# Hybrid decoder block on one core: the down projection's operand sums move into the FFN loop, and the second norm's gain moves to the weights

## The chip, the cores and the metric

The kernel runs on one core of a Trainium2 chip. The time is device microseconds per execution, median of three runs. PE is the matrix engine (TensorE), PEld its weight loads, DVE VectorE, ACT ScalarE, POOL GpSimd, SP the engine whose queue issues most DMAs.

## The reference

One decoder layer in float32 on x of 1024 tokens x 1024: norm, one input projection, retention heads and differential attention side by side, an output projection, then the FFN that this case is about:

```python
x = x + jnp.einsum('bse,ed->bsd', mix, w_out[l])
h2 = rms_norm(x, norm2_g[l])               # norm2_g: one gain for each of the 1024 columns
ff = jax.nn.silu(h2 @ w_gate[l]) * (h2 @ w_up[l])   # 1024 x 2816 each
x = x + ff @ w_down[l]                     # 2816 x 1024
```

## The kernel before

Every large product is made of three matmuls (`mm3`): a float32 operand is cut into `hi`, a cast by ACT to the matrix engine's rounded float32, and `lo`, the rest, subtracted by DVE; hi x hi, hi x lo and lo x hi are summed in PSUM. `wp` holds the moving operands: 8 buffers each of `whi` and `wlo`, and `NRAW` = 2 of the tag `raw` for sums.

The stages on the time axis: projections, attention and retention to about 480 us; the output projection's first column half; then the *middle stage*, about 500 to 617 us: second half of the output projection, token tile by token tile in the order 0, 4, 1, 5, 2, 6, 3, 7, with norm2 and the first gate product between. Its order is written out by hand: `MID_PLAN` gives for a step of the loop over PE's work the functions that are called there (`n_square`: squares on ACT, their sum on POOL; `n_scale`: x2 times 1/norm times `gtile`, on DVE; `n_turn`: transposes on PE; `n_split`: hi and lo of the turned tile; `f_sum`, `f_split`: the sums of quarter blocks that Strassen needs; `g_weights`, `g_add`: the first gate's), and engines keep the program's order there. Elsewhere the scheduler sets the order.

`blk` 0 to 6 hold the seven left operands of the Strassen scheme, turned (0 to 2 in the pool `act2`, 3 to 6 in `act`). In the FFN, 617 to 1024 us, a `Strassen` takes two 128-column tiles of w_gate or w_up: two 512 KB loads (`rawp`, 3 buffers), seven products of 12 matmuls (four k steps by three), five of them with a sum of weights on POOL. Gate and up alternate, 22 in all; silu on ACT, their product on DVE, and the four 128x512 results of a pair go to DRAM (`ffd`).

Down, 1024.5 to 1256.5 us, is Strassen too: `DOWN` lists seven products (n), each 11 steps (c) of 4 token tiles x 3 matmuls, 132. Its a operand comes from `ffd`, its b operand from w_down; `operand` forms the sum of two blocks on POOL if there is one, then hi on ACT and lo on DVE. Five products have an a-sum and five a b-sum, three of them (n = 2, 3, 6) both. w_down's tiles of two of its four quarters are kept (`kept`, 14 slots), the others loaded for each use (`raw`, 5 buffers of the pool `bp`). After each product DVE adds or subtracts the four PSUM banks to one or two of the accumulators `acc`, which start as x2 read back from `x2d`; finished ones go out.

The line number in most rows of the profile is that of the helper which records operations, so groups go by tile names.

Of the kernel before, what the change touches and what calls it, by code (L numbers as in the profile page):

```python
# [25 lines left out]
NF = DFF // P  # L26
# [25 lines left out]
def constants():  # L52
# [148 lines left out]
    (55, "o_load", 3, 1),  # L201
    (55, "o_add", 3, 1),
    (56, "f_split", 3, 2),
    (57, "g_weights", 1),
    (58, "f_sum", 4, 2, "G"),
    (58, "n_square", 3, 1),
# [53 lines left out]
def block_kernel(ctx: ExitStack, tc: tile.TileContext, x, norm1_g, w_in, ret_norm_g, dq_g, dk_g,  # L260
# [4 lines left out]
    class Pinned:  # L265


        def __init__(self, engine):
            self.engine = engine
# [8 lines left out]
    V, A, G, T = Pinned(nc.vector), Pinned(nc.scalar), Pinned(nc.gpsimd), Pinned(nc.tensor)  # L278

    const = ctx.enter_context(tc.tile_pool(name="const", bufs=1))  # L280
    act = ctx.enter_context(tc.tile_pool(name="act", bufs=4))
    wp = ctx.enter_context(tc.tile_pool(name="wp", bufs=KC))
    st = ctx.enter_context(tc.tile_pool(name="st", bufs=6))
# [5 lines left out]
    ident = cs[:, C_ID:C_ID + P]  # L289
    nhalf = cs[:, C_NHALF:C_NHALF + 8]  # L290
    g1col = const.tile([P, KC], F32, name="g1col")
    ms = const.tile([P, NT], F32, name="ms")
    rs = const.tile([P, NT], F32, name="rs")
    eps1 = const.tile([P, NT], F32, name="eps1")
# [49 lines left out]
    def whole(parts):  # L344
        w = next(parts)
        for _ in parts:
            pass
        return w
# [137 lines left out]
    def small_loads():  # L486
        for g_sb, g_dr in ((gq, dq_g), (gk, dk_g)):
            for m in range(2):
                nc.sync.dma_start(g_sb[m * HD:(m + 1) * HD, :], g_dr[0].rearrange("(d o) -> d o", o=1))
        for i, l_dr in enumerate((lq1, lq2, lk1, lk2)):  # L490
            nc.sync.dma_start(lam4[:, i, :], l_dr[0].partition_broadcast(P))
        nc.sync.dma_start(gout[:, 0:4], ret_norm_g[0].rearrange("h d -> (h d)").rearrange("(k p) -> p k", p=P))
        nc.sync.dma_start(gout[:, 4:5], subln_g[0].rearrange("(d o) -> d o", o=1))

    lsum = const.tile([P, 2], F32, name="lsum")
    lexp = const.tile([P, 2], F32, name="lexp")
# [387 lines left out]
    hps = ctx.enter_context(tc.tile_pool(name="hps", bufs=4, space=bass.MemoryType.PSUM))  # L884
    dram = ctx.enter_context(tc.tile_pool(name="dram", bufs=1, space=bass.MemoryType.DRAM))
    x2d = dram.tile([S, D], F32, name="x2d")
    ffd = dram.tile([NF, P, S], F32, name="ffd")
    apx = ExitStack()
    ap = apx.enter_context(tc.tile_pool(name="ap", bufs=2))
    gtile = ap.tile([P, D], F32, tag="rawp", name="gtile", bufs=3)  # L890
    nc.scalar.dma_start(gtile, norm2_g[0].partition_broadcast(P))

    def bankh():
        return hps.tile([P, 512], F32, tag="h", name="h")
# [31 lines left out]

    def n_scale(t, q):
        h2[t] = x2[t]
        V.scalar_tensor_tensor(out=h2[t][q], in0=x2[t][q], scalar=sums[t][:, 0:1],
                               in1=gtile[:, q * 512:(q + 1) * 512], op0=ALU.mult, op1=ALU.mult)  # L930

    def n_turn(t, q):
        turned[t, q] = turn(h2[t][q])
# [39 lines left out]
    class Strassen:  # L973


        def __init__(self, w, f0, pool, tag):
            self.raw, self.w, self.m, self.out, self.pool, self.tag = [], {}, {}, {}, pool, tag
            for j in range(2):
                r = ap.tile([P, 4, 2, P], F32, tag="rawp", name="rawp", bufs=3)
                nc.sync.dma_start(r.rearrange("p k i e -> p k (i e)"),  # L980
                                  w[0, j * 512:(j + 1) * 512, f0 * P:(f0 + 2) * P].rearrange("(k p) e -> p k e", p=P))
                self.raw.append(r)

        def weights(self, n):
            (i, j), other, op, *_ = PRODUCTS[n]
# [53 lines left out]
    def g_load():  # L1039
        gate.append(Strassen(w_gate, 0, rowb, "rowb"))  # L1040

    def g_weights(n):
        gate[0].weights(n)

# [11 lines left out]
    o_load(0, 1)  # L1056
    order["pinned"] = True
    for step, _ in enumerate(mid()):
        if step == 8 * 6:
            g_load()  # L1060
        for at, f, *args in MID_PLAN:
            if at == step:
                names[f](*args)
# [2 lines left out]
            names[f](*args)  # L1066
    order["pinned"] = False

    for f0 in range(0, NF, 2):
# [11 lines left out]
    bp = ctx.enter_context(tc.tile_pool(name="bp", bufs=1))  # L1081
    NH = NF // 2
    keep = act2.tile([P, 8, 512], F32, tag="act2", name="keep")
    more = act2.tile([P, 8, 512], F32, tag="act2", name="more")
    kept = [keep[:, i, :] for i in range(8)] + [more[:, i, :] for i in range(4)]
    kept += [bp.tile([P, 512], F32, name=f"kept{i}") for i in range(2)]
    ff = [more[:, 4:6, :], more[:, 6:8, :]]
    for f in range(2, NF, 4):
        ft = (act2 if f == 2 else act).tile([P, 4, 2, 512], F32, tag="act2" if f == 2 else "act", name="ff")
        ff += [ft[:, i] for i in range(4)]  # L1090
    acc = [[None, None] for _ in range(NT)]

    def w_get(to, c, j, dh):
        f = 2 * c + j
        nc.sync.dma_start(to, w_down[0, f * P:(f + 1) * P, dh * 512:(dh + 1) * 512])
        return to

    def a_get(c, sh, j):
        f = 2 * c + j
        nc.sync.dma_start(ff[f][:, sh, :], ffd[f, :, sh * 512:(sh + 1) * 512])  # L1100

    def operand(both, x_, y_=None, op=None):
        hi, lo = (wp.tile([P, 512], F32R, tag=tag_, name=tag_) for tag_ in ("whi", "wlo"))
        if y_ is not None:
            G.tensor_tensor(out=both, in0=x_, in1=y_, op=op)
# [6 lines left out]
    DOWN = [(((1, 1), None, None), (1, 1), ((1, 0), (0, 0), ALU.subtract), {(0, 0): 1, (1, 0): 1}, ()),  # L1112
            (((1, 0), (1, 1), ALU.add), (1, 0), ((0, 0), None, None), {(1, 0): 1, (1, 1): -1}, ((1, 0),)),
            (((1, 0), (0, 0), ALU.subtract), (0, 0), ((0, 1), (0, 0), ALU.add), {(1, 1): 1}, ()),
            (((0, 0), (1, 1), ALU.add), None, ((1, 1), (0, 0), ALU.add), {(0, 0): 1, (1, 1): 1}, ()),
            (((0, 0), (0, 1), ALU.add), (0, 1), ((1, 1), None, None), {(0, 0): -1, (0, 1): 1}, ()),
            (((0, 0), None, None), None, ((0, 1), (1, 1), ALU.subtract), {(0, 1): 1, (1, 1): 1}, ((0, 1), (1, 1))),
            (((0, 1), (1, 1), ALU.subtract), None, ((1, 0), (1, 1), ALU.add), {(0, 0): 1}, ((0, 0),))]
    at = {}
    for n, ((a0, a1, aop), new, (b0, b1, bop), outs, done) in enumerate(DOWN):  # L1120
        m = [bankh() for _ in range(4)] if n % 2 == 0 else [bankp(), bankp(), bankm([P, 512]), bankm([P, 512])]
        for c in range(NH):

            b = {}
            for name in (b0, b1):
                if name in ((0, 0), (1, 1)):
                    if (name, c) not in at:
                        at[name, c] = w_get(kept[(c if name == (0, 0) else NH + c) % len(kept)], c, *name)
                    b[name] = at[name, c]
                elif name is not None:  # L1130
                    b[name] = w_get(bp.tile([P, 512], F32, tag="raw", name="raw", bufs=5), c, *name)
            if new is not None:
                a_get(c, *new)
            a = {i: ff[2 * c + i[1]][:, i[0], :] for i in (a0, a1) if i is not None}
            both = aop and bp.tile([P, 512], F32, tag="sum", name="sum", bufs=2)
            ah, al = operand(both, a[a0], a.get(a1), aop)
            both = bop and wp.tile([P, 512], F32, tag="raw", name="sum", bufs=NRAW)
            bh, bl = operand(both, b[b0], b.get(b1), bop)
            for t in range(4):
                mm3(m[t], ah[:, t * P:(t + 1) * P], al[:, t * P:(t + 1) * P], bh, bl, c == 0, c == NH - 1)  # L1140
        if n == 0:
            for sh, dh in ((0, 0), (1, 0), (1, 1), (0, 1)):
                for t in range(4 * sh, 4 * sh + 4):
                    acc[t][dh] = (rowb if dh else rowa).tile([P, 512], F32, tag="rowb" if dh else "rowa", name="acc")
                    nc.sync.dma_start(acc[t][dh], x2d[t * P:(t + 1) * P, dh * 512:(dh + 1) * 512])
        for t in range(4):
            for (sh, dh), sign in outs.items():
                o = acc[4 * sh + t][dh]
# [29 lines left out]
```

## Time and profile before

| | |
|---|---|
| median of 3 runs | 1263.63 us (1262.44 to 1264.25) |
| profiled execution, its own time | 1264.15 us |
| its span, first to last instruction | 1262.4 us |
| mean granted TensorE clock | 0.991 |
| busy in the span: PE, DVE, ACT, POOL | 97%, 68%, 43%, 48% |
| DMA | 105.54 MB, mean 84 GB/s |

The page's 40 slices (31.6 us each, busy tenths) show the stages: DVE is full at slices 18 and 19 and from slice 33 on, POOL from 33 on, and the DMA peaks where down begins:

```profile
PE   8999999999999999997999999999999999988998
DVE  6888888845444454378866555555555588999798
ACT  6756566643222232255443434434334333333342
POOL 2655555535444441045543333333333256898576
DMA  6100111102111114321223222232222399321032
```

A group row reads: engine, operation, tile written <- tiles read, size, count | busy us, mean ns of one | idle of that engine before them, with what ended it. A matmul that waits for its successor's data still counts as busy, so the matmuls in a stretch say more than PE's share.

### The profile page before, as it was taken

The numbers are of one execution on the slowest core, as the hardware profiler recorded it, in microseconds if no ns is written. First come the engines' busy times: TensorE is split into PE (matmuls) and PEld (weight loads), VectorE is DVE, ScalarE is ACT, GpSimd is POOL, SyncE is SP. The second block draws the span as 40 slices with busy tenths as digits, with TensorE's granted clock in tenths as the row PEclk, the third lists the DMA queues.
The fourth block names the chain that finished last, engine by engine and source line by source line (L and its number), as shares of the span: only waits on it lengthen the run. The fifth ranks groups of instructions, "written<-read, shape, count | busy, mean of one in ns | idle before, by whom it ended". The sixth has DMA issues, their size and how long they took to land.

```text
span 1262.4 us, 17219 instructions
## 1 busy us (share of the span) xinstructions
PE 1227.2 (97%) x5944; PEld 1023.2 (81%) x5944; DVE 857.4 (68%) x1478; ACT 539.5 (43%) x1194; POOL 601.7 (48%) x732
## 2 busy tenths in 40 slices
PE   8999999999999999997999999999999999988998
PEld 7899999888888888875788888888888887765886
DVE  6888888845444454378866555555555588999798
ACT  6756566643222232255443434434334333333342
POOL 2655555535444441045543333333333256898576
PEclk9999999999999999998899999999999999999999
DMA  6100111102111114321223222232222399321032
GB/s 200 60 26 28 31 30 34 35 1 76 34 42 34 43 59 150 101 83 34 77 90 101 84 84 71 66 99 84 84 84 71 130 309 365 104 82 34 17 125 84
DMA packets 90903, 105.54 MB, mean 84 GB/s; under 512 B 8256, under 2 KB 59584, under 8 KB 90816
## 3 DMA queue, kind: packets, MB, share of 16 engines
q1 hardware_dynamic: 89344, 103.44, 25.8%
q10 hardware_dynamic: 1472, 1.00, 0.3%
q8 instruction: 47, 0.77, 0.2%
q14 instruction: 40, 0.33, 0.1%
HBM read 84.50 MB, written 19.92 MB: 83 GB/s over the span
## 4 chain that ended last, share of the span: by engine, by line
PE 76%; DVE 15%; DMA 3%; issue 2%; ACT 1%; POOL 1%; SPq 0%; POOLq 0%; ACTq 0%; DVEq 0%
PE pp L273 36%; PE h L273 18%; PE m L273 17%; DVE wlo L273 9%; PE big L273 3%; DVE acc L273 2%; DVE act L273 2%; PE o L273 1%; PE it L273 1%; DMA p<-in_x_dram 1%; DVE x L273 1%; POOL sum L273 1%; DMA acc<-x2d 1%; DMA raw<-in_w_in_dram 1%; DMA more<-ffd 0%
## 5 line engine op out<-in xcount | busy, mean ns | idle before, releaser
L273 PE MATMUL pp<-whi,act 128*128 128x512 f32 (+1 forms) x1280 | 415.9, 382 | 1.0 <-ACT act L273 0.7
L273 DVE TENSOR_TENSOR wlo<-sum,whi 128x512 fp32r<-128x512 f32 x220 | 246.9, 1144 | 51.6 <-ACT whi L273 51.2
L273 POOL TENSOR_TENSOR sum<-rawp 128x512 f32<-128x512 f32 x110 | 152.6, 1389 | 249.8 <-DVE wlo L273 247.9
L273 ACT CAST whi<-sum 128x512 fp32r<-128x512 f32 x220 | 136.0, 621 | 302.9 <-POOL sum L273 109.9
L273 PEld LDWEIGHTS pp<-whi,act 128*128 128x128 f32 x1280 | 239.5, 189 | 30.2 <-ACT act L273 0.9
L273 PE MATMUL pp<-wlo,act 128*128 128x512 f32 (+1 forms) x640 | 236.6, 370 | 0.2 <-DVE wlo L273 0.2
L273 PE MATMUL h<-act,whi 128*128 128x512 f32 x584 | 183.0, 394 | 1.4 <-ACT whi L273 1.4
L273 PEld LDWEIGHTS pp<-wlo,act 128*128 128x128 f32 x640 | 121.3, 189 | 13.2 <-DVE wlo L273 0.5
L273 PEld LDWEIGHTS h<-act,whi 128*128 128x128 f32 x584 | 109.7, 188 | 27.2 <-ACT whi L273 1.9
L273 PE MATMUL h<-act,wlo 128*128 128x512 f32 x292 | 114.6, 392 | 0.0
L273 PE MATMUL m<-act,whi 128*128 128x512 f32 x328 | 104.7, 399 | 2.9 <-DVE act L273 2.9
L273 PE MATMUL pp<-act,whi 128*128 128x512 f32 x320 | 103.7, 405 | 2.5 <-DVE act L273 2.2
L273 POOL TENSOR_TENSOR sum<-ff 128x512 f32<-128x512 f32 x50 | 83.0, 1659 | 18.7 <-DVE wlo L273 16.5
L273 DVE TENSOR_TENSOR c<-c,h 128x512 f32<-128x512 f32 x84 | 55.7, 684 | 48.5 <-PE h L273 43.0
L273 PE MATMUL h<-wlo,whi 128*128 128x512 f32 x176 | 71.6, 407 | 8.1 <-DVE wlo L273 8.1
L273 PEld LDWEIGHTS m<-act,whi 128*128 128x128 f32 x328 | 62.3, 190 | 18.2 <-DVE act L273 3.9
L273 PEld LDWEIGHTS pp<-act,whi 128*128 128x128 f32 x320 | 61.9, 193 | 17.7 <-DVE act L273 2.5
L273 POOL TENSOR_TENSOR sum<-raw,keep 128x512 f32<-128x512 f32 x32 | 52.6, 1646 | 41.4 <-DVE wlo L273 24.3
L273 PE MATMUL h<-whi,wlo 128*128 128x512 f32 x176 | 69.7, 396 | 0.0
L273 PE MATMUL h<-whi 128*128 128x512 f32 x176 | 69.6, 395 | 0.0
L273 PEld LDWEIGHTS h<-act,wlo 128*128 128x128 f32 x292 | 54.9, 188 | 12.8
L273 PE MATMUL m<-act,wlo 128*128 128x512 f32 x164 | 65.1, 397 | 0.0
(168 smaller groups left out, 2263.5 us busy)
## 6 DMA issues: line engine op xcount, KB each, us to landing
rawp<-in_w_gate_dram SPq DMA_DIRECT2D x22, 512.0 KB, 3.8
rawp<-in_w_up_dram SPq DMA_DIRECT2D x22, 512.0 KB, 3.9
ffd<-c SPq DMA_DIRECT2D x44, 256.0 KB, 2.0
raw<-in_w_down_dram SPq DMA_DIRECT2D x44, 256.0 KB, 2.7
ff<-ffd SPq DMA_DIRECT2D x40, 256.0 KB, 5.4
raw<-in_w_in_dram SPq DMA_DIRECT2D x32, 256.0 KB, 2.8
raw<-in_w_in_dram SPq DMA_DIRECT2D x26, 192.0 KB, 2.5
p<-in_x_dram SPq DMA_DIRECT2D x8, 512.0 KB, 5.4
```

The source lines that it names most:

```text
L273: i = getattr(self.engine, op)(*args, **kw)
```

## The change

In the FFN loop POOL forms the five a-sums of `DOWN` for each pair (`fsum`, two buffers) and all seven a operands of the pair are stored: `ffd` is 7 x 11 tiles, 77 stores for 44. Down reads them through a ring of eight tiles and never sums on the a side. All 44 tiles of w_down are loaded once and stay (48 slots in `act` and `act2` buffers, taken as the last Strassen's blocks come free); 22 loads and the pool `bp` go. The accumulators' loads are spread over the first three products (`STARTS`). The gain of norm2 goes to the weights: `g2col` holds it by row, `Strassen.gain` multiplies the four 128x256 pieces of a raw tile in place on ACT, eight per Strassen, and `n_scale` becomes an ACT activation with the row's scale. `gtile` and its load go; the first gate's loads are issued 8 steps earlier. A tile `edge` of 96 bytes per partition stands at the right end of the memory and `g2col` (32 bytes) at the left, so the pools behind them start elsewhere.

```diff
+    (54, "g_gain", 1),
+    (56, "g_gain", 0),
...
+    edge = ctx.enter_context(tc.tile_pool(name="edge", bufs=1, side="right")).tile([P, 24], F32, name="edge")
...
+    g2col = const.tile([P, KC], F32, name="g2col")
...
+        nc.sync.dma_start(g2col, norm2_g[0].rearrange("(k p) -> p k", p=P))
...
-    ffd = dram.tile([NF, P, S], F32, name="ffd")
+    ffd = dram.tile([7, NH, P, 512], F32, name="ffd")
-    gtile = ap.tile([P, D], F32, tag="rawp", name="gtile", bufs=3)
-    nc.scalar.dma_start(gtile, norm2_g[0].partition_broadcast(P))
...
     def n_scale(t, q):
         h2[t] = x2[t]
-        V.scalar_tensor_tensor(out=h2[t][q], in0=x2[t][q], scalar=sums[t][:, 0:1],
-                               in1=gtile[:, q * 512:(q + 1) * 512], op0=ALU.mult, op1=ALU.mult)
+        A.activation(h2[t][q], x2[t][q], AF.Copy, scale=sums[t][:, 0:1])
...
+        def gain(self, j):
+            for k in range(4):
+                A.activation(self.raw[j][:, k], self.raw[j][:, k], AF.Copy, scale=g2col[:, 4 * j + k:4 * j + k + 1])
...
         def whole(self):
+            for j in (1, 0):
+                self.gain(j)
             for n in range(7):
...
-        if step == 8 * 6:
+        if step == 8 * 5:
             g_load()
...
             V.tensor_tensor(out=u_, in0=u_, in1=g[i, sh], op=ALU.mult)
-            nc.sync.dma_start(ffd[f0 + i, :, sh * 512:(sh + 1) * 512], u_)
+        for n, ((a0, a1, aop), *_) in enumerate(DOWN):
+            src = up[a0[1], a0[0]]
+            if a1 is not None:
+                both = ap.tile([P, 512], F32, tag="sum", name="fsum", bufs=2)
+                G.tensor_tensor(out=both, in0=src, in1=up[a1[1], a1[0]], op=aop)
+                src = both
+            nc.sync.dma_start(ffd[n, f0 // 2], src)
...
+    slots = []
+    for i in range(7):
+        pool, tag = ((act2, "act2"), (act, "act"))[i % 2 if i < 6 else 1]
+        wide = pool.tile([P, 8, 512], F32, tag=tag, name="wide")
+        slots += [wide[:, j, :] for j in range(8)]
+    ring, kept = slots[:8], slots[8:]
...
+            b = [w_get(c, *name) for name in (b0, b1) if name is not None]
+            ah, al = operand(a_get(n, c))
+            bh, bl = operand(*b, bop) if bop else operand(*b)
```

Three places in the engines' order. POOL first. Before, in down's fourth product (n = 3), an a-sum (`ff` or `more`) and a b-sum stand in turn at every c:

```order
L273 TENSOR_TENSOR sum<-more 128x512
L273 TENSOR_TENSOR sum<-more,keep 128x512
L273 TENSOR_TENSOR sum<-ff 128x512
L273 TENSOR_TENSOR sum<-kept_10480,keep 128x512
L273 TENSOR_TENSOR sum<-ff 128x512
L273 TENSOR_TENSOR sum<-kept_10481,keep 128x512
```

Now, from the last two FFN pairs to the end, `sum<-rawp` being a weight sum of a Strassen and `sum<-wide` a b-sum of down:

```order
L275 TENSOR_TENSOR sum<-rawp 128x512 x9
L275 TENSOR_TENSOR fsum<-c 128x512 x4
L275 TENSOR_TENSOR sum<-rawp 128x512
L275 TENSOR_TENSOR fsum<-c 128x512
L275 TENSOR_TENSOR sum<-rawp 128x512
L275 TENSOR_TENSOR sum<-wide 128x512 x6
L275 TENSOR_TENSOR fsum<-c 128x512 x4
L275 TENSOR_TENSOR sum<-wide 128x512
L275 TENSOR_TENSOR fsum<-c 128x512
L275 TENSOR_TENSOR sum<-wide 128x512 x48
```

Down keeps 55 sums of its 110; the other 55 stand in the FFN, those of the last pair behind the sixth and the seventh b-sum of down.

DVE in the middle stage, before, around the norm of token tiles 2 and 6 (`x` rows are x2's halves, `act_6332` and the like are blocks in `act2`):

```order
L273 SCALAR_TENSOR_TENSOR x_6310<-x_6310,sso,gtile 128x512
L273 SCALAR_TENSOR_TENSOR x_6810<-x_6810,sso,gtile 128x512
L273 TENSOR_TENSOR act<-sum,act 128x512
L273 TENSOR_TENSOR x_6881<-pp,xr 128x512
L273 TENSOR_TENSOR act_6332<-sum,act_6332 128x512
L273 TENSOR_TENSOR sum<-x_6571,x_6630 128x512
L273 TENSOR_TENSOR act_6330<-h,act_6330 128x512
L273 SCALAR_TENSOR_TENSOR x_6461<-x_6461,sso,gtile 128x512
L273 SCALAR_TENSOR_TENSOR x_6881<-x_6881,sso,gtile 128x512
```

Now ACT has these scalings, and the gains of the first gate's weights ahead of their casts:

```order
L275 COPY x_6818<-h 128x512
L275 ACTIVATE sq,sso<-x_6885 128x512
L275 CAST act_6334<-h 128x512
L275 COPY x_6316<-h 128x512
L275 ACTIVATE x_6465<-x_6465,sso 128x512
L275 ACTIVATE x_6885<-x_6885,sso 128x512
L275 CAST act<-sum 128x512
L275 ACTIVATE sq,sso<-x_6494 128x512
L275 CAST act<-sum 128x512
L275 COPY x_6465<-h 128x512
L275 CAST act_6335<-h 128x512
L275 COPY x_6885<-h 128x512
```

```order
L275 ACTIVATE rawp<-rawp,g2col 128x256 x4
L275 CAST act<-sum 128x512
L275 ACTIVATE rawp<-rawp,g2col 128x256 x4
L275 CAST whi<-rawp 128x512
L275 ACTIVATE sq,sso<-x_6954 128x512
```

The scalings moved from DVE's row to ACT's, two for each token tile, and the eight gains are new there.

SP's queue at the start of down, now (`ffd<-fsum` stores a sum of the last pair, `wide<-ffd` loads an a operand):

```order
L1106 DMA ffd<-c 128x512
L1159 DMA acc<-x2d 128x512
L1127 DMA wide<-in_w_down_dram 128x512
L1106 DMA ffd<-c 128x512
L1106 DMA ffd<-fsum 128x512 x2
L1127 DMA wide<-in_w_down_dram 128x512
L1133 DMA wide<-ffd 128x512
L1106 DMA ffd<-fsum 128x512 x2
```

Before, the same stretch held loads and only the last pair's plain stores:

```order
L1095 DMA keep<-in_w_down_dram 128x512
L1076 DMA ffd<-c 128x512
L1100 DMA more<-ffd 128x512
L1100 DMA ff<-ffd 128x512
L1095 DMA raw<-in_w_down_dram 128x512
L1095 DMA keep<-in_w_down_dram 128x512
```

Stores that wait for POOL's sums have come between the loads of w_down.

More of the change, by code (lines that the diff above doesn't have):

```diff
@@ L886, in block_kernel @@
     x2d = dram.tile([S, D], F32, name="x2d")
-    ffd = dram.tile([NF, P, S], F32, name="ffd")
+    NH = NF // 2
+    ffd = dram.tile([7, NH, P, 512], F32, name="ffd")
     apx = ExitStack()
     ap = apx.enter_context(tc.tile_pool(name="ap", bufs=2))
-    gtile = ap.tile([P, D], F32, tag="rawp", name="gtile", bufs=3)
-    nc.scalar.dma_start(gtile, norm2_g[0].partition_broadcast(P))
     def bankh():
@@ L1040, in g_load, with g_gain @@
         gate.append(Strassen(w_gate, 0, rowb, "rowb"))
+    def g_gain(j):
+        gate[0].gain(j)
     def g_weights(n):
@@ L1067, in block_kernel @@
     order["pinned"] = False
+    DOWN = [(((1, 1), None, None), ((1, 0), (0, 0), ALU.subtract), {(0, 0): 1, (1, 0): 1}, ()),
+            (((1, 0), (1, 1), ALU.add), ((0, 0), None, None), {(1, 0): 1, (1, 1): -1}, ((1, 0),)),
+            (((1, 0), (0, 0), ALU.subtract), ((0, 1), (0, 0), ALU.add), {(1, 1): 1}, ()),
+            (((0, 0), (1, 1), ALU.add), ((1, 1), (0, 0), ALU.add), {(0, 0): 1, (1, 1): 1}, ()),
+            (((0, 0), (0, 1), ALU.add), ((1, 1), None, None), {(0, 0): -1, (0, 1): 1}, ()),
+            (((0, 0), None, None), ((0, 1), (1, 1), ALU.subtract), {(0, 1): 1, (1, 1): 1}, ((0, 1), (1, 1))),
+            (((0, 1), (1, 1), ALU.subtract), ((1, 0), (1, 1), ALU.add), {(0, 0): 1}, ((0, 0),))]
     for f0 in range(0, NF, 2):
@@ L1075, in block_kernel @@
             V.tensor_tensor(out=u_, in0=u_, in1=g[i, sh], op=ALU.mult)
-            nc.sync.dma_start(ffd[f0 + i, :, sh * 512:(sh + 1) * 512], u_)
-    apx.close()
[L1081 to L1090, printed above, removed]
-    acc = [[None, None] for _ in range(NT)]
-    def w_get(to, c, j, dh):
-        f = 2 * c + j
-        nc.sync.dma_start(to, w_down[0, f * P:(f + 1) * P, dh * 512:(dh + 1) * 512])
-        return to
-    def a_get(c, sh, j):
-        f = 2 * c + j
-        nc.sync.dma_start(ff[f][:, sh, :], ffd[f, :, sh * 512:(sh + 1) * 512])
@@ new lines, in block_kernel, with w_get, a_get @@
+    ring, kept = slots[:8], slots[8:]
+    n_ring = [0]
+    acc = [[None, None] for _ in range(NT)]
+    at = {}
+    def w_get(c, j, dh):
+        if (c, j, dh) not in at:
+            f = 2 * c + j
+            to = at[c, j, dh] = kept[len(at)]
+            nc.sync.dma_start(to, w_down[0, f * P:(f + 1) * P, dh * 512:(dh + 1) * 512])
+        return at[c, j, dh]
+    def a_get(n, c):
+        to = ring[n_ring[0] % len(ring)]
+        n_ring[0] += 1
+        nc.sync.dma_start(to, ffd[n, c])
+        return to
@@ L1103, in operand @@
+    def operand(x_, y_=None, op=None):
         hi, lo = (wp.tile([P, 512], F32R, tag=tag_, name=tag_) for tag_ in ("whi", "wlo"))
         if y_ is not None:
+            both = wp.tile([P, 512], F32, tag="raw", name="sum", bufs=NRAW)
             G.tensor_tensor(out=both, in0=x_, in1=y_, op=op)
@@ L1109, in operand @@
         return hi, lo
[L1112 to L1118, printed above, removed]
@@ L1119, in block_kernel @@
-    at = {}
-    for n, ((a0, a1, aop), new, (b0, b1, bop), outs, done) in enumerate(DOWN):
+    STARTS = [((0, 0), (1, 0)), ((1, 1),), ((0, 1),)]
+    for n, (_, (b0, b1, bop), outs, done) in enumerate(DOWN):
         m = [bankh() for _ in range(4)] if n % 2 == 0 else [bankp(), bankp(), bankm([P, 512]), bankm([P, 512])]
         for c in range(NH):
[L1124 to L1138, printed above, removed]
@@ new lines, in block_kernel @@
+            b = [w_get(c, *name) for name in (b0, b1) if name is not None]
+            ah, al = operand(a_get(n, c))
+            bh, bl = operand(*b, bop) if bop else operand(*b)
+            if n < len(STARTS) and c >= NH - 8:
+                sh, dh = STARTS[n][(c - NH + 8) // 4] if len(STARTS[n]) > 1 else STARTS[n][0]
+                if len(STARTS[n]) > 1 or c >= NH - 4:
+                    t = 4 * sh + (c - NH + 8) % 4
+                    acc[t][dh] = (rowb if dh else rowa).tile([P, 512], F32, tag="rowb" if dh else "rowa", name="acc")
+                    nc.sync.dma_start(acc[t][dh], x2d[t * P:(t + 1) * P, dh * 512:(dh + 1) * 512])
@@ L1139, in block_kernel @@
             for t in range(4):
                 mm3(m[t], ah[:, t * P:(t + 1) * P], al[:, t * P:(t + 1) * P], bh, bl, c == 0, c == NH - 1)
[L1141 to L1145, printed above, removed]
         for t in range(4):
```

1 line of the change is left out of this document (removed).

## The prediction

> **What bounds the kernel now.** I read the page first, then windows by stage, then the waits, the groups and the chain of the stages that lose time. The page has PE at 97%:
>
> ```profile
> PE 1227.2 (97%) x5944; PEld 1023.2 (81%) x5944; DVE 857.4 (68%) x1478; ACT 539.5 (43%) x1194; POOL 601.7 (48%) x732
> ```
>
> That share hides losses, since a matmul that waits for its successor still counts, so I count matmuls per window (columns: stretch, length, PE, PEld, DVE, ACT, POOL, granted clock, DMA share, GB/s). The first rows are down's, the last the middle stage's and the FFN's:
>
> ```profile
> 1024.50:1054.45 29.95, 29.95 (x133) 24.77 (x132) 25.40 (x27) 13.85 (x24) 18.48 (x12) 1.00 0.98 347
> 1050.00:1100.00 50.00, 48.99 (x214) 39.48 (x212) 49.79 (x50) 19.99 (x36) 37.87 (x25) 1.00 0.63 223
> 1100.00:1150.00 50.00, 43.81 (x177) 31.98 (x177) 50.00 (x35) 18.54 (x30) 49.31 (x30) 1.00 0.22 69
> 1150.00:1200.00 50.00, 45.27 (x184) 35.89 (x183) 41.10 (x49) 18.37 (x32) 29.48 (x19) 0.93 0.07 21
> 1200.00:1262.00 62.00, 56.61 (x243) 44.66 (x241) 56.50 (x49) 21.15 (x35) 44.28 (x27) 1.00 0.32 107
> ...
> 560.00:580.00 20.00, 17.09 (x83) 13.10 (x81) 18.28 (x22) 12.21 (x27) 12.19 (x15) 0.99 0.17 59
> 580.00:600.00 20.00, 14.33 (x50) 10.07 (x51) 17.38 (x18) 9.78 (x19) 12.01 (x10) 0.84 0.13 39
> 600.00:620.00 20.00, 18.03 (x63) 13.84 (x62) 18.13 (x21) 9.74 (x17) 11.34 (x8) 0.83 0.25 66
> 620.00:640.00 20.00, 20.00 (x88) 16.22 (x87) 17.23 (x23) 8.37 (x16) 11.18 (x8) 1.00 0.44 133
> 700.00:800.00 100.00, 100.00 (x434) 81.15 (x433) 58.71 (x89) 38.46 (x67) 35.91 (x26) 1.00 0.28 85
> ```
>
> Three readings. Down's first product (132 matmuls) takes 29.95 us at PE's own rate, 0.227 us a matmul; 50 us should hold 220, and 1100 to 1200 holds 177 and 184. There DVE is busy for 50.00 of 50. In the FFN PE never pauses, with DVE at 59% and POOL at 36%. In the middle stage, where norm2 runs between the last output projections and the first gate, DVE is at 87 to 91% and PE gives 50 and 63 matmuls where 88 fit.
>
> What ties DVE to POOL in down shows in its groups (to 1262), beside the same operations in the FFN (650 to 990):
>
> ```profile
> L273 DVE TENSOR_TENSOR wlo<-sum,whi 128x512 fp32r<-128x512 f32 x99 | 149.5, 1557 | 9.6 <-ACT whi L273 9.6
> L273 POOL TENSOR_TENSOR sum<-ff 128x512 f32<-128x512 f32 x50 | 83.0, 1659 | 18.7 <-DVE wlo L273 16.5 <-DMA ff<-ffd 2.2
> ...
> L273 DVE TENSOR_TENSOR wlo<-sum,whi 128x512 fp32r<-128x512 f32 x88 | 60.4, 686 | 35.8 <-ACT whi L273 35.8
> L273 POOL TENSOR_TENSOR sum<-rawp 128x512 f32<-128x512 f32 x89 | 121.9, 1370 | 223.0 <-DVE wlo L273 223.0
> L273 ACT CAST whi<-sum 128x512 fp32r<-128x512 f32 x88 | 54.7, 622 | 147.7 <-PE h L273 67.1 <-PE pp L273 41.5 <-PE m L273 39.1
> ```
>
> One subtraction is 0.69 us alone and 1.56 us where POOL adds without pause: they take turns. With two POOL sums per c (one of the 11 steps of a product), a step costs two turns, about 2 x 1.70 = 3.4 us, against 12 x 0.227 = 2.72 us of PE. With one sum per c the timeline of 1201 to 1206 gives the step directly:
>
> ```profile
> 1201.29 1.69 POOL L273 TENSOR_TENSOR sum<-raw,keep 128x512 f32<-128x512 f32 x1 [0.63 <-DVE wlo L273]
> 1203.60 1.68 POOL L273 TENSOR_TENSOR sum<-raw,keep 128x512 f32<-128x512 f32 x1 [0.63 <-DVE wlo L273]
> 1205.90 1.68 POOL L273 TENSOR_TENSOR sum<-raw,keep 128x512 f32<-128x512 f32 x1 [0.63 <-DVE wlo L273]
> ```
>
> 2.31 us, below 2.72: such a product follows PE. The chain says the same, DVE carrying the products with two sums (columns: start, us, what):
>
> ```profile
> 1055.77 4.86 DVE acc L273 x8
> ...
> 1090.74 35.17 DVE wlo L273 x22
> ...
> 1128.31 25.15 DVE wlo L273 x17
> ...
> 1229.59 23.32 DVE wlo L273 x15
> ...
> 1256.48 2.73 DVE acc L273 x4
> ```
>
> **Part 1: the a-sums leave down.** Down runs from 1024.50 to the last accumulate at 1256.48: 231.98 us. Seven products at 29.95 are 209.65, so 22.3 us are lost, all in products that form an a-sum. After the change no product has more than one sum per c: 2.31 x 11 = 25.4 us, plus 4.86 us for eight accumulates, 30.3 us of DVE against 29.95 of PE, and products without a sum (n = 1 and 4) stand between. I take all 22.3 as removed; the 0.93 of granted clock in 1150 to 1200 lies in it. DVE is 0.3 us late per product at worst, next in line.
>
> **Part 2: the sums in the FFN.** 55 sums come to POOL. 100 us hold 2.57 gate and up pairs, 12.9 sums x 1.37 to 1.66 = 18 to 21 us: POOL goes from 36 to 57%, DVE from 59 to at most 71% if each of its subtractions beside them is held by 0.9 us. PE stays the bound with eight whi buffers ahead of it (a Strassen's seven products, 19.4 us). Cost 0. The 33 added stores (77 for 44, 256 KB) are 8.7 MB in 408 us, 21 GB/s on 85: hidden too. At the boundary the last five fsums stand in POOL's row between down's first sums, and their stores stand on SP's queue ahead of w_down's loads for c = 6 to 9. Five sums are 8.3 us and a load lands after 2.7 us:
>
> ```profile
> raw<-in_w_down_dram SPq DMA_DIRECT2D x44, 256.0 KB, 2.7
> acc<-x2d SPq DMA_DIRECT2D x16, 256.0 KB, 5.9
> rawp<-in_w_gate_dram SPq DMA_DIRECT2D x22, 512.0 KB, 3.8
> ```
>
> That stretch already moves 347 GB/s at a DMA share of 0.98, so I put 1.5 us there (0 to 5.9, one such landing missed). The rest of down's DMA moves less: 137 transfers of 256 KB for 126, but 22 w_down loads fewer in the later products, where the share is at most 0.63.
>
> **Part 3: the gain.** DVE's 16 scalings go, and ACT gets 16 of 128x512 and 8 of 128x256 ahead of the first gate's weights. Rows of the middle stage, and of operations with a per-partition scale:
>
> ```profile
> L273 DVE SCALAR_TENSOR_TENSOR x<-x,sso,gtile 128x512 f32<-128x512 f32 x16 | 14.7, 937 | 7.3 <-POOL sso L273 5.6 <-DMA x2d<-x 1.6
> L273 ACT ACTIVATE whi<-raw,gout 128x512 fp32r<-128x512 f32 x16 | 11.2, 722 | 21.8 <-PE pp L273 21.8
> L273 ACT ACTIVATE q<-m,gq 128x256 fp32r<-128x256 f32 x32 | 15.2, 474 | 18.2 <-PE m L273 18.2
> ...
> 576.47 1.68 DVE x L273
> ...
> 585.09 1.76 DVE x L273
> ```
>
> DVE loses 14.7 us, ACT gains 16 x 0.72 + 8 x 0.47 = 15.3 us, where it was at 49 to 61%. In the two windows from 580 to 620 PE falls 38 and 25 matmuls short of 620's 88: 14.3 us. A scaling on the chain was up to 1.76 and becomes 0.72, and what queued on DVE behind it comes earlier; but norm, turn, split, sum stay in series and ACT stands in that series too (turned copies, casts). Ends: ACT's 8 gains and waits cost 3 us more than DVE gives back (+3); two thirds of the 14.3 come back (-10). I take -5, a third, since DVE's share of work there falls by about a third of its excess over PE.
>
> On the clock: it was 0.84 and 0.83 in these two windows. The Trainium skill, "TensorE: Matmul & The Clock Gate", section "What's actually happening", has the clock halved after an idle window of about 3.4 us; by it a middle stage without such windows would win up to 40 x 0.165 = 6.6 us more, as an estimate. The trace's PE waits there are short of that, so the rule isn't the term of the sum.
>
> Gains of the other 21 Strassens: 8 x 0.47 = 3.8 us of ACT per 19.4 us. ACT goes from 38% to 58%. The raw tile takes 3.8 us to land, its gain follows, and only then POOL sums it; ACT's row holds casts behind a waiting gain. By the instruction order I follow a lateness of up to 7.5 us, within the lead of 19.4. Cost 0, with rows of cover: ACT idle 147.7 us for PE. The 512 KB load of gtile and the new 4 KB one are hidden.
>
> **Part 4: addresses.** Two small tiles shift every pool: wp's tiles (moving operands of projections and down) go from a multiple of 64 bytes to 32 off, the blocks in act likewise, those in act2 the other way. The FFN's chain shows two rates for the same 12 matmuls; the slow one is on blocks in act2 (32 off now), the fast one on act:
>
> ```profile
> 691.49 2.72 PE h L273 x12
> 694.21 2.81 PE pp L273 x12
> 697.03 2.76 PE h L273 x12
> ```
>
> A Strassen has three slow and four fast blocks, and then four and three: +0.09 x 22 = +2.0 us. In the projections and down (x768, x384 and x924 of 512 columns) the price is between 0 and 0.09 / 12 = 7.8 ns a matmul:
>
> ```profile
> L273 PE MATMUL pp<-whi,act 128*128 128x512 f32 x768 | 261.4, 402 | 0.0
> L273 PE MATMUL pp<-wlo,act 128*128 128x512 f32 x384 | 149.8, 390 | 0.0
> ```
>
> 2076 x 7.8 is 16 us. I take a quarter, 2 ns, 4.1 us (2.3 and 1.8): a row of these operands is one piece of 2 KB, where a row of the FFN's blocks is four pieces of 512 bytes, and the trace doesn't separate the address from other differences between the blocks.
>
> **The sum.** The profiled execution is 1264.15 us (span 1262.4), 0.5 above the median. 1264.15 - 22.3 + 1.5 - 5 + 2.0 + 4.1 = 1244.45; less 0.5 for the median: 1244.
>
> **Rivals.**
> (a) DVE and POOL still bound down: the accumulates delay the next product's subtractions as in 1229.59, and the single-sum products lose half of what the double ones did: 11 us back, 1255. For it: 30.3 against 29.95. Against: the two products that form only a b-sum (first and sixth) ran at PE's rate.
> (b) The middle stage turns its DVE wait into an ACT wait: 5 to 8 us worse than forecast, 1249 to 1252. For it: turned copies already wait on ACT for DVE. Against: ACT's 49%.
> (c) The addresses cost the full 7.8 ns: 1244 + 12 = 1256; or nothing, with a larger middle gain: 1237.
> (d) Slower: the FFN starves. Loads, gains, sums and casts form one series per Strassen, with three raw tiles; if a waiting gain holds ACT's row so that the lateness passes 19.4 us, each later Strassen pays. At 1.5 us each, 21 cost 31 us: 1275, and the point at which it eats the gain is 20 / 21 = 0.95 us each. Five fsums that hold DVE add up to 8.3 us per pair to that lateness. The Trainium skill, "SBUF — State Buffer", section "Terms", speaks for this: DVE and GpSimd hold their shared ports exclusively, the loser blocks fully; down's 1557 against 686 agrees. Against: 7.5 + 8.3 is 15.8, still below 19.4, and all engines but PE keep 29% or more of each 100 us.
>
> **How the numbers follow.** Forecast (1238 to 1250) 0.60; (a) 0.12; (b) 0.09; (c) dear 0.05, free 0.05; (d) 0.09, of which slower 0.08. The range takes the forecast, (b), the free end of (c) and most of (a): 1236 to 1255. Within 0.2% (2.5 us, about what a measurement can tell from no change) needs a loss of just 17 to 22 us: 0.03. Faster is the rest, 0.89.
>
> **What would show it.** Down's windows at 217 or more matmuls per 50 us, wlo<-sum below 1.3 us on average there, and no long chain pieces of DVE wlo (part 1). From 650 to 990 PE without idle, POOL near 57% and ACT near 58% (parts 2, 3). Between 560 and 620 DVE below 80%, and the first gate ending about 5 us sooner (part 3). Two rates in the FFN swapped, 2.81 four times per Strassen, and the first down product at 30.2 (part 4). PE idle on ACT whi in the FFN, or whi waiting for a raw tile's landing, would make it wrong.

## The result, and the profile after

The changed kernel takes 1247.96 us (1246.93 to 1248.67, four runs) against 1263.14 for the kernel before in the same rounds: ratio 0.9878, 95% interval 0.9861 to 0.9896. The profiled execution is 1247.36 us, its span 1245.5, 16.9 less than before. The forecast was 1244 with 1236 to 1255. Two executions in all were slow, one of the kernel before (1498 us) and one of the run with the stores on GpSimd's queue (2434 us), and stand in none of the times and ratios here.

The start times of PE's stages say where the 16.9 us came from. They are read from the trace's matmuls and counted from the first matmul, not from the span's start, 1.4 us earlier:

| us | before | after | difference |
|---|---|---|---|
| first gate begins | 579.94 | 585.48 | +5.5 |
| first gate's duration | 34.92 | 31.29 | -3.6 |
| first up to down (FFN) | 408.24 | 406.56 | -1.7 |
| down, first product | 29.92 | 36.81 | +6.9 |
| down, the other six, to the last matmul | 203.64 | 179.94 | -23.7 |
| last matmul begins | 1256.65 | 1240.08 | -16.6 |

Windows of the kernel after, with the columns of the table in the prediction:

```profile
560.00:580.00 20.00, 16.89 (x80) 13.12 (x78) 9.97 (x12) 15.19 (x35) 8.69 (x10) 1.00 0.19 66
580.00:600.00 20.00, 13.23 (x49) 10.02 (x50) 13.27 (x15) 12.84 (x26) 11.41 (x12) 0.83 0.04 14
600.00:620.00 20.00, 16.82 (x64) 12.76 (x63) 19.84 (x23) 13.92 (x28) 12.82 (x9) 0.91 0.18 53
700.00:800.00 100.00, 100.00 (x435) 81.47 (x435) 73.52 (x91) 54.39 (x114) 52.18 (x37) 1.00 0.29 93
1000.00:1050.00 50.00, 45.49 (x195) 36.44 (x194) 30.57 (x39) 15.63 (x28) 26.46 (x19) 0.99 0.73 253
1100.00:1150.00 50.00, 50.00 (x223) 41.39 (x222) 44.16 (x44) 22.54 (x39) 28.20 (x19) 1.00 0.37 105
1150.00:1200.00 50.00, 50.00 (x222) 41.42 (x221) 38.85 (x53) 21.31 (x37) 12.84 (x9) 1.00 0.32 95
```

From 1100 PE has 222 and 223 matmuls per 50 us where it had 177 and 184: full rate. The new loss stands in 1000 to 1050, with 195. In the middle stage DVE fell from 18.28 to 9.97 of 20 us and from 17.38 to 13.27, and PE's matmuls didn't rise: 80, 49, 64 for 83, 50, 63. From 600 to 620 DVE is as full as before, 19.84 for 18.13. PE's own waits name what took DVE's place (engine and tile, what was waited for: us, times, longest). Before, from 555 to 620 us:

```profile
PE h L273 <- ACT whi L273: 3.1, 2, 1.7
PE m L273 <- DVE act L273: 2.9, 3, 1.6
PE h L273 <- DVE x L273: 2.3, 5, 1.0
PE pp L273 <- DVE act L273: 2.2, 1, 2.2
```

After, from 500 us to the end:

```profile
PE h L275 <- ACT x L275: 9.5, 5, 4.5
PE h L275 <- ACT whi L275: 4.4, 1, 4.4
```

The waits on DVE in the middle stage fell from 7.4 us to 4.4 (two rows of 2.2 on its `act`, not shown), and those on ACT rose from 3.4 (0.3 of it in a row that isn't shown) to 9.5. The first row after is the turns of x2's halves waiting for ScalarE's scalings, the second the stall in down's first product. That stall in the chain, start, us, what:

```profile
1030.18 1.68 POOL sum L275
1031.86 1.71 POOL fsum L275
1033.58 2.00 DMA ffd<-fsum
1035.72 1.84 POOL fsum L275
1037.58 3.28 DMA ffd<-fsum
...
1043.46 3.99 DMA wide<-ffd
1048.20 1.30 DVE wlo L275 x2
1049.55 6.77 PE h L275 x23
```

The last pair's five sums wait for their two buffers' stores, an a load stands on SyncE's queue behind the fifth store, and PE waits for that load. And the FFN's products, which the prediction had as 2.81 and 2.72, before the change:

```profile
693.09 2.72 PE h L275 x12
695.81 2.80 PE pp L275 x12
698.61 2.75 PE h L275 x12
```

The slow ones are still those on the blocks in act2, although these now stand on a multiple of 128.

### The profile page after: what moved, and what is told of

The parts are those of the page before. It is cut to its first block, busy times and chain, and to the rows that moved or that the text cites. A ratio compares the mean times of both kernels' runs of the same rounds, so it can differ in the third digit from the quotient of the medians.

```text
span 1245.5 us, 17506 instructions
## 1 busy us (share of the span) xinstructions
PE 1214.5 (98%) x5944; PEld 1020.4 (82%) x5944; DVE 847.1 (68%) x1462; ACT 605.4 (49%) x1386; POOL 589.9 (47%) x732
## 4 chain that ended last, share of the span: by engine, by line
PE 83%; DVE 7%; DMA 3%; ACT 3%; issue 1%; POOL 1%; SPq 0%; DVEq 0%; ACTq 0%; POOLq 0%
PE pp L275 38%; PE h L275 23%; PE m L275 18%; PE big L275 2%; DVE act L275 2%; DVE wlo L275 2%; PE o L275 1%; PE it L275 1%; DMA p<-in_x_dram 1%; ACT x L275 1%; DVE acc L275 1%; DMA rawp<-in_w_up_dram 1%; ACT act L275 1%; DVE q L275 1%; POOL sso L275 0%
## 5 line engine op out<-in xcount | busy, mean ns | idle before, releaser
L275 DVE TENSOR_TENSOR wlo<-sum,whi 128x512 fp32r<-128x512 f32 x165 | 187.9, 1139 | 90.9 <-ACT whi L275 90.3
L275 ACT ACTIVATE rawp<-rawp,g2col 128x256 f32<-128x256 f32 x176 | 78.6, 501 | 141.3 <-DMA rawp<-in_w_gate_dram 90.7
L275 POOL TENSOR_TENSOR sum<-wide 128x512 f32<-128x512 f32 x55 | 83.6, 1520 | 131.3 <-DVE wlo L275 107.2
L275 ACT CAST whi<-sum 128x512 fp32r<-128x512 f32 x165 | 100.7, 616 | 46.0 <-POOL sum L275 45.6
L275 DVE TENSOR_TENSOR wlo<-wide,whi 128x512 fp32r<-128x512 f32 x99 | 76.3, 795 | 45.3 <-ACT whi L275 45.2
L275 ACT CAST whi<-wide 128x512 fp32r<-128x512 f32 x99 | 59.2, 621 | 97.2 <-PE m L275 43.7
L275 POOL TENSOR_TENSOR fsum<-c 128x512 f32<-128x512 f32 x55 | 85.6, 1564 | 11.0 <-DMA ffd<-fsum 11.0
L275 DVE TENSOR_TENSOR wlo<-rawp,whi 128x512 fp32r<-128x512 f32 x44 | 61.5, 1397 | 15.3 <-ACT whi L275 15.3
L275 PE MATMUL h<-wlo,whi 128*128 128x512 f32 x176 | 69.1, 393 | 0.0
```

The costliest lines, as they stand in the source:

```text
L275: i = getattr(self.engine, op)(*args, **kw)
```

## The experiments

Each was timed in at least three rounds against the kernel before; a stage is read from its profile. Stage times repeat well in the FFN and in down; in the middle stage two kernels with the same code there differ by up to 3 us, so a single difference below that proves nothing there, and the sign is taken from all the profiles together.

**Down's part alone.** The changed kernel with the gain's hunks undone:

```diff
-        A.activation(h2[t][q], x2[t][q], AF.Copy, scale=sums[t][:, 0:1])
+        V.scalar_tensor_tensor(out=h2[t][q], in0=x2[t][q], scalar=sums[t][:, 0:1],
+                               in1=gtile[:, q * 512:(q + 1) * 512], op0=ALU.mult, op1=ALU.mult)
...
-            for j in (1, 0):
-                self.gain(j)
```

> The changed kernel without the gain's part: gtile, its load and the scaling with gain on VectorE as before, no gains on ScalarE; down's operands stored and w_down kept as in the change. Theory A (the gain's part cost some 2 us, in the early gains on ScalarE near 480 us and in the middle stage, and the whole saving is down's): the first up product begins some 2 us sooner than after the change, the FFN and down take the same, so about 1246. Rival B (VectorE's relief did help the middle stage and the 2 us are lost elsewhere, by the moved addresses): slower than after the change, 1249 to 1253.

Measured 1238.51 us, 0.9806 (0.9792 to 0.9821). Theory A has the sign, and not the size: 9.5 us less than the changed kernel. The first up product begins at 614.61 instead of 616.77; the FFN, which A left alone, is 6.7 us shorter. Its chain reads:

```profile
692.37 2.72 PE pp L273 x12
695.09 2.72 PE h L273 x12
```

All products at 2.72, 19.04 us a Strassen. This kernel has the edge tile and no g2col, so nothing at the left end has moved.

**The gain alone**, on the kernel before (the same hunks, with g2col and without the edge):

> The kernel before with the gain's part alone (gains on ScalarE in the FFN, scaling of x2's rows on ScalarE), down as it was. Theory A: 1 to 3 us slower than before, 1264 to 1266, with the loss between 480 and 617 us and none in the FFN (19.4 us a Strassen). Rival B: 2 to 5 us faster than before.

Measured 1263.88 us, 1.0001 (0.999 to 1.0012): no difference. The first up product begins at 616.85 (614.85 before) as A has it, and the FFN gives 2.4 back from there to down (386.40 for 388.80 in the 20 Strassens behind the first up, and 0.1 in that one), which neither had. Its products take 2.76 and 2.77, so the addresses, again, do something that is not in either theory.

**Scaling back on VectorE**, by a row factor alone:

```diff
-        A.activation(h2[t][q], x2[t][q], AF.Copy, scale=sums[t][:, 0:1])
+        V.tensor_scalar(out=h2[t][q], in0=x2[t][q], scalar1=sums[t][:, 0:1], scalar2=None, op0=ALU.mult)
```

> The changed kernel with the 16 scalings of x2's rows back on VectorE, as a tensor_scalar by the row's factor; the gains stay on ScalarE. Theory A1 (ScalarE's queue in the middle stage is what the turned tiles wait for: 9.5 us of PE's waits are on it): these waits go, the first gate begins 3 to 5 us sooner, the first up product 2 to 5 us sooner, 1243 to 1246. Rival A2 (the eight gains ahead of the first gate's casts are the cost): the first up product begins when it did, within 1 us, 1247 to 1248.

Measured 1244.39 us, 0.9846 (0.983 to 0.9863), a time inside A1's bounds. The first gate begins 3.5 us sooner (581.99), as A1 has it, the first up product 1.8 us (614.98), just short of its 2. The wait on ACT's x is gone and another stands there:

```profile
PE h L275 <- DVE x L275: 5.8, 2, 4.8
```

One scaling is 671 ns here, 721 ns on ScalarE and 937 ns before, so 50 ns of length is not what decides; what is left is the row in which the scaling queues, which the waits bear out.

**Stores of the last pair on GpSimd's queue.**

```diff
-            nc.sync.dma_start(ffd[n, f0 // 2], src)
+            queue = nc.gpsimd if f0 == NF - 2 and a1 is not None else nc.sync
+            queue.dma_start(ffd[n, f0 // 2], src)
```

> The changed kernel with the last pair's five summed stores issued from GpSimd's queue instead of SyncE's, where loads of down's first product stood behind them. Theory C (the 4.55 us stall near 1044 and the half-rate matmuls behind it come from those stores on SyncE's queue): the first product of down falls from 36.8 to 30 or 31 us, 1241 to 1243. Rival D (the sums on GpSimd themselves, or the DMA's rate, hold the first product): it stays above 34 us and the time within 2 us of 1248.

Measured 1247.72 us, 0.9875 (0.9858 to 0.9891); the first product 37.39 us. Theory C fell, and D's first half is what the timeline of GpSimd shows:

```profile
1033.39 3.44 POOL L275 TENSOR_TENSOR fsum<-c 128x512 f32<-128x512 f32 x2
1036.77 1.36 POOL L1107 DMA_DIRECT2D ffd<-fsum  x2
1038.14 1.31 POOL L275 TENSOR_TENSOR sum<-wide 128x512 f32<-128x512 f32 x1
1042.38 1.28 POOL L275 TENSOR_TENSOR fsum<-c 128x512 f32<-128x512 f32 x1 [2.93 <-DMA ffd<-fsum]
```

The next b-sum of down (`sum<-wide`) follows only at 1046.71, behind two more sums and their stores. So SyncE's queue was not the only place in which the same step was late.

**No edge tile.**

```diff
-    edge = ctx.enter_context(tc.tile_pool(name="edge", bufs=1, side="right")).tile([P, 24], F32, name="edge")
```

> The changed kernel without the tile edge of 96 bytes, so that the three blocks in act2 start 96 bytes off a multiple of 128 again, as before the change. The theory of the prediction (the address sets the rate): a product on these blocks goes from 2.80 to 2.86 us or more, the FFN 2 us or more slower. Rival (the address is worth a hundredth of a us, the place or the order of the blocks sets the rate): 2.80 becomes 2.81 as before, the FFN 0.5 to 1.6 us slower, the time within 2 us of 1248.

Measured 1247.48 us, 0.986 (0.9845 to 0.9874). Neither: a Strassen is 19.32 instead of 19.36, faster, with 2.76 and 2.77 where the changed kernel has 2.80 and 2.75. The blocks in act2 are 96 bytes off a multiple of 128 here, those in act and the weights 32. Before, act2 was 96 off as well, the weights 0 off, and the same products took 2.81. So the rate of one block changed with the address of the other operand.

**The order of the products**, in each Strassen after the first (a copy on ACT and an addition on DVE change places between two products with it; not shown):

```diff
-            for n in range(7):
+            for n in (0, 2, 4, 1, 3, 5, 6):
```

> The changed kernel with the seven products of each Strassen after the first in another order: the three whose blocks lie in act2 first, then the four in act. If the slow 2.80 us belongs to the blocks in act2, three products stay at 2.80, one follows at 2.74 and three take 2.72: 19.31 us a Strassen in place of 19.36, 1 us less in all. If it belongs to a product's place in the order (every second one), the rates stay in the places 1, 3 and 5 and 19.36 stays.

Measured 1256.76 us, 0.9946 (0.9927 to 0.9964). On the question asked it is clear, the rates go with the blocks:

```profile
695.62 2.80 PE pp L275 x12
698.42 2.80 PE h L275 x12
701.22 2.80 PE m L275 x12
704.02 2.75 PE h L275 x12
```

With the three on act2 in a row, the second and third stay slow though no block in act stands between. But the kernel is 9 us slower: at the end of the FFN PE waits 5.6 us on ACT's whi, and the first product of down takes 40.24. By the trace's times a weight's `wlo` ends 7 us ahead of its product here on average, falling to about zero in the last pairs; in the changed kernel it is 11 us ahead. Why the order costs the weights that lead wasn't followed further.

**Each gain twice.** The 21 later Strassens get a second pass in place, by 1.0:

```diff
             for j in (1, 0):
                 self.gain(j)
+                self.gain(j, 1.0)
```

> The changed kernel with a second ScalarE pass over each weight tile of the 21 later Strassens (a copy in place by the factor 1.0, eight more of 128x256), so ScalarE has 8 x 0.50 = 4.0 us more per 19.36 us. If the FFN has the slack that the prediction counted (a lateness of 7.5 us of 19.4), nothing changes: 19.36 us a Strassen, 1247 to 1249. If the series of load, gain, sum and cast was near its end, PE waits on ScalarE in the FFN and each Strassen takes 1 us or more longer: 1268 or more.

Measured 1267.58 us, 1.0024 (1.0012 to 1.0035). The FFN's slack is less than 4 us of ScalarE per Strassen: 20 of them take 402.70 us for 387.20, 0.78 more on average. The loss isn't spread evenly. The first eight of the later ones still take 19.36 us; from then on every second one, an up, takes 0.3 to 5.1 us more. A window of this kernel shows ScalarE far from full while PE falls short of 435:

```profile
700.00:800.00 100.00, 98.19 (x426) 79.40 (x425) 60.73 (x78) 62.29 (x145) 49.61 (x36) 1.00 0.29 93
```

So no engine's share is the limit; by exclusion it is the series load, gain, sum, cast, subtraction. The lead of `wlo` over its product, averaged, is 17 us before the change, 11 after, 3.5 here with moments below zero: the lead is a stock, and PE pays once it is used up.

**All operands 32 bytes off.**

```diff
-    edge = ctx.enter_context(tc.tile_pool(name="edge", bufs=1, side="right")).tile([P, 24], F32, name="edge")
+    edge = ctx.enter_context(tc.tile_pool(name="edge", bufs=1, side="right")).tile([P, 16], F32, name="edge")
```

> The changed kernel with the tile edge at 64 bytes in place of 96, so that the blocks in act2 stand 32 bytes off a multiple of 128, as the blocks in act and the weights (whi, wlo) do since the change. Theory E (a matmul is slow where its two operands' addresses differ modulo 128, not where one of them is off a boundary): all seven products take 2.72 us, a Strassen 19.04, 6.5 to 7 us less in all, 1241. Rival F (an operand has to stand on a multiple of 64 or 128 by itself): the blocks in act2 get slower or stay at 2.80, 1248 or more.

The mechanism is E's: with nothing on a multiple of 64, every product takes 2.72.

```profile
691.07 2.72 PE m L275 x12
693.79 2.72 PE h L275 x12
```

The FFN is 6.7 us shorter (399.84 for 406.56), and the time is 1246.86 us, 0.9869 (0.9853 to 0.9886), not 1241: the first product of down takes 41.71 us where it took 36.81, and ends at 1060.30, where it ended at 1060.14. By these times what feeds that product didn't come sooner, and 4.9 us of the gain went into the wait there. The middle stage took 2.0 us more in this profile.

**The last pair's sums late.** On down's part alone, the five sums, their stores and four accumulator loads stand behind down's first product:

```diff
+            if f0 == NF - 2 and a1 is not None:
+                late.append((n, src, up[a1[1], a1[0]], aop))
+                continue
...
+        if n == 0:
+            late_sums()
+            start(1, 0, range(4, 8))
```

> Down's part alone (as in the run without the gain's part), with the last pair's five sums, their stores and four loads of accumulators put in the program behind down's first product. Theory G (GpSimd's row and SyncE's queue together hold down's first product: its b-sums stand behind the last pair's sums, which wait for their two buffers' stores, and its loads behind those stores): the first product falls from 36.4 to 30 to 32 us, 1232 to 1235. Rival D (the DMA's rate at the start of down holds it): it stays above 35 us, 1237 or more.

Measured 1239.08 us, 0.9814 (0.9797 to 0.983), no gain over down's part alone. The first product falls to 29.92 us, as G has it and below its 30, and the second rises from 30.94 to 37.36: the a loads of the second now stand behind those stores. So G holds for the product and not for the time. The chain's piece, start, us, what:

```profile
1037.70 1.33 POOL fsum L273
1039.05 1.99 DMA ffd<-fsum
1041.17 1.29 POOL fsum L273
1043.89 5.95 DMA wide<-ffd
```

In GpSimd's row the scheduler put five b-sums ahead of the last three of the late sums. SyncE's queue has a gap from 1012.4 to 1019.5 us here, and the first product ran at PE's rate in spite of it (GpSimd's rows first, then SyncE's):

```profile
1025.78 1.74 POOL L273 TENSOR_TENSOR sum<-wide 128x512 f32<-128x512 f32 x1
...
1037.70 3.04 POOL L273 TENSOR_TENSOR fsum<-c 128x512 f32<-128x512 f32 x2 [0.37 <-DMA ffd<-fsum]
...
1011.31 1.10 SPq L1120 DMA_DIRECT2D wide<-in_w_down_dram  x2
1019.49 0.33 SPq L1100 DMA_DIRECT2D ffd<-c  x1
```

**The edge alone**, on the kernel before:

> The kernel before with nothing but the tile edge of 96 bytes at the right end. Theory E: the blocks in act2, those in act and the weights all stand on multiples of 128, a Strassen takes 19.04 us in place of 19.44, 8 to 9 us less over the FFN, 1255. Rival F2 (the FFN's rate has another cause in the runs without the gain's part, such as ScalarE's or the DMA's load): 19.4 stays, 1263.

Measured 1255.75 us, 0.9939 (0.9924 to 0.9954). Theory E: one tile of 96 bytes that nothing reads is worth 7.8 us (1263.55 before in the same rounds). The FFN's products are at 2.72, the FFN is 8.4 us shorter, and down's seven together take what they took (233.5 us for 233.6).

**Late stores on GpSimd's queue**, with three buffers for the sums:

```diff
-            nc.sync.dma_start(ffd[n, NH - 1], both)
+            nc.gpsimd.dma_start(ffd[n, NH - 1], both)
...
-            start(1, 0, range(4, 8))
+            start(1, 0, range(4, 8), nc.gpsimd)
```

> As the run with the late sums, but the five late stores and the four accumulator loads behind them are issued from GpSimd's queue, and the sums of that pool have three buffers for two. Theory G (it is the waits that stand in SyncE's queue ahead of loads, together with the sums ahead of b-sums in GpSimd's row): with nothing that waits on GpSimd left on SyncE, the first two products of down take 60 to 62 us together (67.3 with the late sums on SyncE), 1231 to 1234. Rival D (the DMA's rate): the two stay above 65 us, 1236 or more.

Measured 1236.31 us, 0.9776 (0.9758 to 0.9793). The second product is at 29.92, the first at 37.80: 67.7 together, so by the numbers rival D's forecast came in and G's did not. But GpSimd's row changed too: the last two of the late sums stand ahead of the last four b-sums again, and they wait 2.6 us for a buffer's store. That the DMA's rate alone holds the first product isn't shown either, since it took 29.92 in the run with the late sums. SyncE's timeline has the same gap as there:

```profile
1010.46 1.29 SPq L1120 DMA_DIRECT2D wide<-in_w_down_dram  x2
1018.54 0.33 SPq L1100 DMA_DIRECT2D ffd<-c  x1
```

From 1011.8 to 1018.5 SyncE issues nothing: it stands with the last pair's first plain store, which waits for one of DVE's last multiplications. The chain goes from the last of them through the second plain store and two loads of w_down to a b-sum at 1034.87, and GpSimd's row came free for that sum at the same time.

**The plain stores late as well:**

```diff
+            if n == 0 and c == NH - 1:
+                for n_, x_ in plain:
+                    nc.sync.dma_start(ffd[n_, NH - 1], x_)
             ah, al = operand(a_get(n, c))
```

> As the run before it (late sums and their stores on GpSimd's queue), with the last pair's two plain stores put behind the loads of down's first product, just ahead of the last a load, which needs one of them. In the runs so far SyncE issues nothing for 7 to 8 us, waiting with the first of these stores for VectorE's last multiplications, while a dozen loads of the first product stand behind it. Theory H (that hole is what makes the loads late): the first product falls from 37.8 to 30 to 32 us, 1229 to 1231. Rival D (the DMA's rate, 35 and more transfers in 30 us): it stays above 35 us, 1235 or more.

Measured 1235.11 us, 0.9771 (0.9757 to 0.9784), the fastest of all, though not to be told from the run before it: the middle stage took 3.1 us more in this profile than in that one, with the same code. The gap is gone (the transfers run at 389 GB/s from 1013 to 1023, at 209 in the run before), and the first product is 34.22 us, 3.6 less, neither H's 30 to 32 nor D's 35; the time is D's. How much of the 3.6 us is the gap's stays open: the product began 3.1 us later than in the run before and ended only 0.5 us sooner (1050.31 for 1050.81), and in the run with the late sums on SyncE's queue it took 29.92 with the gap in place. That run also tells against D's rate as the bound. What is left there:

```profile
1025.66 6.25 DVE wlo L273 x3
...
1035.88 1.30 POOL sum L273
...
1037.86 1.68 DVE wlo L273
```

The late sums still stand in GpSimd's row ahead of the last four b-sums, and DVE's subtractions beside them take 2 us each. Of the runs with stored sums, the one that had five b-sums ahead of the last late sums is the one whose first product ran at PE's rate. That order together with stores that hold up no loads wasn't tried.

## Why the prediction was right, and where its steps were not

The time lay in the range, 4 us above the point. Part 1, which carries the gain, was right in mechanism and size. That the rest came so near was luck in good part: the other terms were off by 3.7 to 6.9 us each, two upwards and two downwards. Rival (b) came in, and the addresses cost nothing as at the free end of rival (c).

- **Part 1, the a-sums leave down: right.** -22.3 forecast; the six products behind the first gained 23.7, at PE's rate from down's third on. DVE's groups there (1060 to the end) show one sum in turn with one subtraction, 1430 ns instead of 1557, so the forecast "below 1.3 us on average" was missed, without effect: what counts is that a step has one turn and not two. One thing the step passed over: before, down's fifth product formed an a-sum alone and still took 37.2 us, so one sum per step did not always follow PE; it forms no sum now.

```profile
L275 DVE TENSOR_TENSOR wlo<-sum,whi 128x512 fp32r<-128x512 f32 x44 | 62.9, 1430 | 0.0
```

- **Part 2, the boundary: mis-sized, 1.5 forecast, 6.9 measured.** The step named the sums in POOL's row and the stores on SyncE's queue and took one missed landing, with 5.9 as the upper end. Shown: the five sums stand among down's b-sums in POOL's row and wait there for their stores, and loads stand behind these stores on SyncE's queue. Moving the stores to GpSimd's queue, or the sums behind the b-sums, moves the stall and doesn't shorten it: the first two products take 67.3 or 67.7 us together in all these runs, 67.4 in the changed kernel. The fastest run leaves 4.3 in the first product. Which of the two queues costs how much stays open. PE's clock took its part: behind the 4.4 us stall some six matmuls ran at half the rate, 427 ns each.
- **Part 2, the FFN: right that PE stays the bound** (PE 100.00 of 100, DVE 73.5, ACT 54.4, POOL 52.2; forecast 71, 58, 57). The lateness of up to 7.5 us was right in size, the lead of `wlo` falling by 6 on average. What was missing is that the lead isn't a one-time cost: where PE is faster (all operands 32 off), the lead shrinks from pair to pair to 0.4 us. Rival (d) was nearer than its 0.09 suggests: 4 us more of ScalarE per Strassen is enough (each gain twice).
- **Part 3, the middle stage: wrong, -5 forecast, +1.9 measured.** The step took a third of PE's loss as won with DVE's relief. DVE was relieved, and PE then waited on ScalarE's x for 9.5 us: rival (b), and at its price: the term came out 6.9 us worse than forecast. Over all profiles the first up product begins at 616.8 to 618.8 with the scaling and the gains on ScalarE (seven kernels) and at 613.2 to 616.3 with neither (six), so the sign is shown and the size is 2 to 3 us. 0.9 of it falls between 480 and 510 us. There two early gains that had waited 2.5 us for w_up's load stand ahead of a cast, and PE pauses for 0.7 us behind them, at 485.29, until ACT has written another tile:

```profile
482.98 0.91 ACT L275 ACTIVATE rawp<-rawp,g2col 128x256 f32<-128x256 f32 x2 [2.55 <-DMA rawp<-in_w_up_dram]
483.79 0.56 ACT L275 CAST act<-m 128x512 fp32r<-128x512 f32 x1
```

- **Part 4, the addresses: the mechanism failed.** +2.0 in the FFN and +4.1 elsewhere were forecast from the address of one operand; measured -1.7 and nothing (before 480 us PE is 0.2 us ahead of its times before the change, and down's products that don't wait are at 29.92 in both). What counts is how the two operands stand to each other. In the projections and in down both moved by the same 32 bytes, so nothing changed.
- **The clock.** The prediction set a rule of the Trainium skill ("TensorE: Matmul & The Clock Gate", section "What's actually happening") beside part 3: the clock is halved after an idle window of about 3.4 us. By it a middle stage without such windows would have won up to 6.6 us more, as an estimate. The waits there stayed, longest 4.5 us, the granted clock from 580 to 620 was 0.83 and 0.91 (0.84 and 0.83 before), and no run had full clock through its middle stage, so the estimate was not tested. Before the change no wait from 555 to 620 was longer than 2.2 us, and matmuls ran at half rate there all the same (427 ns each from 610.7 to 613.7), so in this trace it took no single wait of 3.4 us.
- **The sum:** the errors were -1.4, +5.4, +6.9, -3.7 and -4.1, together 3.1 us by the stage times.

## What to carry to other kernels

A term that hides behind slack is read from the series, not from shares: ScalarE at 54% had less than 4 us to give in each 19.4, and the lead of the prepared operand over its product said so before PE lost any time. When a stage that was the bound is unblocked, look first at what stands in the in-order queues ahead of its first loads; here one wait took over from another, and the one that shows is only the latest. And work that was moved off a full engine did not help here, because the engine that took it comes next in the same series.

## What the runs showed of the hardware

The rate of a matmul depends on how its two operands' addresses in a partition stand to each other modulo 128, for the FFN's moving blocks in act2 or act and its weights (whi, wlo), with 12 matmuls of 512 columns. The addresses are those that the built programs give the tiles; the traces hold none.

| kernel | weights, blocks in act, blocks in act2 (bytes off a multiple of 128) | us on act2, on act |
|---|---|---|
| before | 0, 0, 96 | 2.81, 2.76 and 2.72 |
| after | 32, 32, 0 | 2.80, 2.75 and 2.72 |
| no edge; gain alone | 32, 32, 96 | 2.76, 2.77 and 2.72 |
| edge of 64 bytes | 32, 32, 32 | 2.72, 2.72 |
| edge alone; down's part alone | 0, 0, 0 | 2.72, 2.72 |

Where two values stand for act, the first is of a product that follows one on act2, the second of one that follows a product on act: the slow rate carries over some six matmuls. Each matmul took 227 ns where the operands agree and nearly always 231 to 240 through a whole product where they differ by 32, some 3% more. That it is the pair and not one operand is shown by the rows with 32: act at 32 is fast with weights at 32, and act2 at 0 is slow with them, though fast with weights at 0. Modulo 128 the runs hold just two differences, the weights 32 bytes further on (before, after) and 64 apart (no edge; gain alone: 225 to 237 ns). What another difference would cost, 128 bytes among them, and which part of the engine makes it, no run shows.
